# Dilated attention: probabilities and values as f32 operands of one product, instead of f16 halves in three

## The chip, the cores and the metric

The kernel runs on one core of a Trainium2 chip. The metric is the device time of one execution in microseconds (us). The core has a matrix engine (PE, whose weight loads the profile lists apart as PEld), a vector engine (DVE), a scalar engine (ACT), GpSimd (POOL) and a queue engine (SP), each with its own instruction stream; semaphores order them against each other. Matmuls read SBUF and write into the banks of PSUM, and ACT and DVE read those banks out.

## The reference

One residual layer on x of 1024 tokens by 1024 channels, all in f32. A normalised input is projected to 9232 columns; from these come a mixture of three dilated sliding-window attentions (8 heads of 64 in each of three groups), a gated delta rule, and gates that merge the two. The change lies in the attention:

```python
def _dilated_window_attention(q, k, v, window, dilation):
    ...
    scores = jnp.einsum('brnqhd,brnkhd->brnhqk', qb, kb) * (dh ** -0.5)
    ...                                             # causal mask and window
    m = jnp.max(scores, axis=-1, keepdims=True)
    p = jnp.exp(scores - m)
    den = jnp.sum(p, axis=-1, keepdims=True)
    o = jnp.einsum('brnhqk,brnkhd->brnqhd', p / den, vb)
    lse = (m + jnp.log(den))[..., 0].transpose(0, 1, 2, 4, 3)

def _dilated_mixture(q, k, v):
    ...                                             # one call for each of the three groups
    wts = jax.nn.softmax(jnp.stack(lses), axis=0)
    o = jnp.einsum('gbsh,gbshd->bshd', wts, jnp.stack(outs))
```

Queries and keys lie in blocks of 128; a block of queries meets its own block of keys and, where there is one, the block before.

## The kernel before, in words

Large products are made from f16 halves: an f32 operand is split into a high half and the f16 remainder, and three f16 products (high by high, high by low, low by high) are summed in PSUM. The helper `mm3_steps` (lines 183 to 185) issues them for the projections; `STT` and `TT` (lines 83 and 86) are short names of DVE operations, so many groups of the profile bear these two lines and are told apart by their tiles.

The projections are cut into units of 256 columns (q, k or v of four heads, a pair of gate columns, and so on). A `Feed` holds them in a list and hands them out a tick at a time, so that they can be interleaved with other work; a tick is one or a few steps of three products. PE's instructions stand in the order in which the program issues them. The instructions of DVE and ACT are put in order by a scheduler, which goes by priorities and its own estimates of when each can start.

The attention works on sets: a group g and a half of the heads hs, six in all, in the order (2,0), (2,1), (1,0), (1,1), (0,0), (0,1). The projection of a set's values is `v_unit`: for every two blocks of 128 tokens a PSUM bank of 512 columns is read out into `Vh` (by ACT, line 730) and `Vl` (by DVE, through `STT`), both f16. `att_run` goes through a set in 16 steps, one for each block of queries j and parity of the heads, two heads a step. It is a generator; between its parts the feed issues projections of the next units. A step has three parts, which run one step behind the other:

- `scores`: two products a head into a bank of "S" (lines 790 and 792), then on DVE the mask and the row maximum into `sm` (line 799), then on ACT the exponential and its row sums (line 803).
- `turn`: the probabilities are transposed by PE into a bank of "G" (line 813, f32, one turn for each head and block of keys); ACT copies them to `th` in f16 (line 818), and DVE writes the remainder `tl` (through `TT`, so line 86).
- `values`: for each head and each block of keys three products of 128 x 128 weights (`th`, `th`, `tl`) with 64 columns (`Vh`, `Vl`, `Vh`), lines 836, 838 and 840, into the one bank of "O". After the second parity ACT copies the bank to `osb` (line 845).

A block of queries has one block of keys in group 2, in the first block of each of the four strides of group 1, and in the first block of group 0; otherwise two. The results of groups 1 and 2 go to DRAM; in group 0 `combine` reads them back and mixes the three by their denominators, and later turns the result (line 899).

`Vh`, `Vl`, `sm`, `th` and `tl` lie in pools with two buffers a tag. In `rope_first` the slots of the values' tags are also lent to the first keys (`pkh`, `pkl`).

Of the kernel before, what the change touches and what calls it, by code (L numbers as in the profile page):

```python
# [10 lines left out]
F32 = mybir.dt.float32  # L11
F16 = mybir.dt.float16
BF16 = mybir.dt.bfloat16
AF = mybir.ActivationFunctionType
ALU = mybir.AluOpType
# [3 lines left out]
S = 1024  # L19
# [3 lines left out]
H_SCALE = 16.0  # L23
W_SCALE = 256.0
P_SCALE = 1.0 / (H_SCALE * W_SCALE)
# [52 lines left out]
def hybrid_block(ctx: ExitStack, tc: tile.TileContext, A):  # L78
    nc = tc.nc
    V, SC, PE, GP = nc.vector, nc.scalar, nc.tensor, nc.gpsimd  # L80

    def STT(out, in0, scalar, in1, op0, op1, eng=None):
        (eng or V).scalar_tensor_tensor(out, in0, scalar, in1, op0=op0, op1=op1)  # L83

    def TT(out, in0, in1, op, eng=None):
        (eng or V).tensor_tensor(out, in0, in1, op)  # L86
# [9 lines left out]
    start = [ctx.enter_context(ExitStack()) for _ in range(2)]  # L96
# [399 lines left out]
    with tc.manual_schedule(engines={nc.vector.engine, nc.scalar.engine}):  # L496
# [8 lines left out]
        pts = turn_rows(0)  # L505
# [11 lines left out]
        pts = turn_rows(1)  # L517
        split_rows(1, pts)
        rows_product(q, wq, 1, 0)
        pts = turn_rows(2)  # L520
# [12 lines left out]
        pts = turn_rows(3)  # L533
# [45 lines left out]
    ap = att.enter_context(tc.tile_pool(name="att", bufs=1, side="right"))  # L579
# [15 lines left out]
    def rope_room():  # L595
        return rp.tile([128, 2, 512], F32, name="rx", tag="rx", bufs=2)
# [37 lines left out]
    def rope_tiles():  # L634
        return {n: rp.tile([128, 2, S], F16, name=f"pc{n}", tag=f"pc{n}", bufs=1) for n in "hl"}
# [31 lines left out]

    def rope_first(g, ws, pieces):

        pts = [rope_tiles(), {n: ap.tile([128, 2, S], F16, name=f"pk{n}", tag="V" + n, bufs=2) for n in "hl"}]  # L670

        def half(pt, banks, hf, *offset):
            x = rope_room()
            for ct, p in enumerate(banks):
                rope_evict(g, x, p, ct, *offset)
            rope_half(g, pt, hf, x, *offset)

        for pt, banks in zip(pts, qk):
            half(pt, banks, 0, 0)
        ab = [q, [bank("S", 2), bank("S", 2)]]  # L680
        for i, u in ((2, 1), (3, 0), (3, 1)):
            for ct in range(2):
                quarter(ab[u][ct], ws[u], ct, i)
            if u == 0:

                with tc.high_priority():
                    for n in range(2):
                        feed.units[0][1].split(n)
        for pt, banks in zip(pts, ab):
            half(pt, banks, 1)  # L690
        for pt, pc in zip(pts, pieces):
            rope_out(pt, pc)
# [16 lines left out]

    def v_unit(g, tiles):  # L710
        def start():
            vs = [ap.tile([128, 8, 256], F16, name=n, tag=n, bufs=2) for n in ("Vh", "Vl")]
            tiles().extend(vs)
            return vs

        def gen(w):
            wh, wl = w
            Vh, Vl = start()
            for jj in range(4):
                p = bank("mm", 3)  # L720
                for u in range(2):
                    j = 2 * jj + u
                    for i, _ in enumerate(mm3_steps(
                            p[:, u * 256:u * 256 + 256], (lambda k: tok(g, h_hi, k, j), lambda k: tok(g, h_lo, k, j)),
                            (lambda k: wh[:, k], lambda k: wl[:, k]), first=(u == 0))):
                        if u == 1 and i == KT - 1:
                            with tc.high_priority():
                                vh = Vh[:, 2 * jj:2 * jj + 2].rearrange("p a b -> p (a b)")
                                vl = Vl[:, 2 * jj:2 * jj + 2].rearrange("p a b -> p (a b)")
                                SC.activation(vh, p, AF.Copy, scale=H_SCALE * P_SCALE)  # L730
                                STT(vl, p, H_SCALE * P_SCALE, vh, ALU.mult, ALU.subtract)
                        if i % 2:
                            yield

        def gen7(w):
            vs = start()

            def out(c, hf, p, rest):
                cs = slice(128 * c, 128 * c + 128)
                vh, vl = [v[:, 4 * hf:4 * hf + 4, cs] if g == 0 else  # L740
                          v.rearrange("p (r h) c -> p r h c", h=2)[:, :, hf, cs] for v in vs]
                p = p.rearrange("p (i c) -> p i c", c=128)
                with tc.high_priority():
                    if rest is not None:
                        rest = rest.rearrange("p (i c) -> p i c", c=128)
                        x = rope_room()[:, 0].rearrange("p (i c) -> p i c", c=128)
                        STT(x, p, -1.0, rest, ALU.mult, ALU.subtract)
                        p = x
                    SC.activation(vh, p, AF.Copy, scale=H_SCALE * P_SCALE)
                    STT(vl, p, H_SCALE * P_SCALE, vh, ALU.mult, ALU.subtract)  # L750

            yield from seven_products(w, out, by_token(g))

        return gen, gen7
# [2 lines left out]

    def att_run(g, hs, ts, pace):

        Qh, Ql, K, Vh, Vl = ts  # L760
        steps = [(j, par) for j in range(8) for par in range(2)]
        osbs, Ps, ths, pos = {}, {}, {}, {}
        if (g, hs) == sets[-1]:

            room = ap.tile([128, 2048], F32, name="osbs", tag="Ks", bufs=2)
# [40 lines left out]
        def turn(s):  # L806
            nk = len(blocks(steps[s][0]))
            P = Ps.pop(s)
            pt = bank("G", 2)
            for u in range(2):  # L810
                for i in range(nk):
                    c = (u * nk + i) * 128
                    PE.transpose(pt[:, c:c + 128], P[:, u, i * 128:i * 128 + 128], ident)  # L813
            n = 256 * nk
            th = ap.tile([128, 512], F16, name="th", tag="th", bufs=2)
            tl = ap.tile([128, 512], F16, name="tl", tag="tl", bufs=2)
            with tc.high_priority():
                SC.copy(th[:, :n], pt[:, :n])  # L818
                TT(tl[:, :n], pt[:, :n], th[:, :n], ALU.subtract)
            ths[s] = th, tl  # L820

        def values(s):
            j, par = steps[s]
            kb = blocks(j)
            nk = len(kb)
            th, tl = ths.pop(s)
            if par == 0:
                pos[j] = bank("O", 1)
            po = pos[j]
            for u in range(2):  # L830
                hd = 2 * u + par
                out = po[:, hd * 64:hd * 64 + 64]
                vs = slice(hd * 64, hd * 64 + 64)
                for i, b in enumerate(kb):
                    c = slice((u * nk + i) * 128, (u * nk + i) * 128 + 128)
                    PE.matmul(out, lhsT=th[:, c], rhs=Vh[:, b, vs], start=(hd == 0 and i == 0), stop=False,
                              skip_group_check=True)
                    PE.matmul(out, lhsT=th[:, c], rhs=Vl[:, b, vs], start=False, stop=False,
                              skip_group_check=True)
                    PE.matmul(out, lhsT=tl[:, c], rhs=Vh[:, b, vs], start=False, stop=(i == nk - 1),  # L840
                              skip_group_check=True)
            if par == 0:
                return
            osb = osbs.pop(j)
            SC.copy(osb[:, :256], po[:, :256])
            if g == 1:
                dst = dram[g, hs].rearrange("(n r) c -> r n c", r=4)[j // 2, 128 * (j % 2):128 * (j % 2) + 128]
                nc.scalar.dma_start(out=dst, in_=osb)
            elif g == 2:
                nc.scalar.dma_start(out=dram[g, hs].rearrange("(n r) c -> r n c", r=8)[j], in_=osb)  # L850
            else:
                feed.later(TURN_LAG, combine(hs, j, osb))

        n = len(steps)
# [11 lines left out]
    def combine(hs, j, osb):  # L866
# [8 lines left out]
        f = ap.tile([128, 3, 4], F32, name="f", tag="f", bufs=2)  # L875
        mx = ap.tile([128, 3, 4], F32, name="mx", tag="mx", bufs=2)
# [5 lines left out]
        TT(mx[:, 1], sml[:, 0], sml[:, 1], ALU.add)  # L882
        TT(mx[:, 1], mx[:, 1], sml[:, 2], ALU.add)
        V.reciprocal(mx[:, 2], mx[:, 1])
        STT(f, f, 1.0 / H_SCALE, mx[:, 2:3].to_broadcast([128, 3, 4]), ALU.mult, ALU.mult)

        def hv(x):
            return x.rearrange("p (h v) -> p h v", v=64)
# [88 lines left out]
    tiles = {}  # L977
# [93 lines left out]
    for t in range(8):  # L1071
        tk = slice(t * 128, t * 128 + 128)
        for k in range(KT):
            PE.matmul(pba[:, t * 32:t * 32 + 32], lhsT=h_hi[:, k, tk], rhs=wbas[:, k], start=(t == 0 and k == 0),
                      stop=False, skip_group_check=True)
            PE.matmul(pba[:, t * 32:t * 32 + 16], lhsT=h_lo[:, k, tk], rhs=wbas[:, k, 0:16], start=False,
                      stop=(k == KT - 1), skip_group_check=True)
# [595 lines left out]
    for t in range(8):  # L1673
# [373 lines left out]
```

## Time and profile before

| | |
|---|---|
| median of 3 runs | 1074.25 us (1074.08 to 1074.3) |
| profiled execution, its time | 1076.42 us |
| profiled execution, its span | 1074.6 us |
| mean granted clock of PE | 0.997 |
| attention steps (first turn to last value product) | 101.5 to 545.3 us |
| busy in the span | PE 1048.8, PEld 640.7, DVE 864.8, ACT 560.9, POOL 56.3 us |

The profile is of one execution. Each engine's busy time is the union of its instructions' records. A group is one line, engine, operation and pair of tiles, written as out<-in with its shape (partitions x elements) and type; behind it stand how often it ran, its busy time, the mean duration of one, and how long its engine was idle just before, with what ended that idle time. In the views in order of time a row gives the start, the duration, and the instructions that were merged into it. Line numbers are those of the kernel before.

### The profile page before, as it was taken

To read this page: it belongs to the slowest core of one execution; us is meant where nothing else is said; L and a number is where in the kernel's file an instruction comes from. 1 tells how busy PE (TensorE), PEld (TensorE's weight loads), DVE (VectorE), ACT (ScalarE), POOL (GpSimd) and SP (SyncE) were. 2 spreads that over 40 slices of the span, in tenths; PEclk is the share of its full clock that TensorE was granted. 3 is DMA by queue.
4 is the path that set the end of the run, shared out by engine and by line. 5 is a ranking of instruction groups with operands and counts; after the bars stand their busy time and mean duration, and the time that the engine had idled before them with its cause. 6 is when DMAs were issued, how large, how long until landed. Compare 5 with 4: busy or idle time off the path is not lost.

```text
span 1074.6 us, 23700 instructions
## 1 busy us (share of the span) xinstructions
PE 1048.8 (98%) x9410; PEld 640.7 (60%) x9410; DVE 864.8 (80%) x1986; ACT 560.9 (52%) x1274; POOL 56.3 (5%) x107
## 2 busy tenths in 40 slices
PE   7999999999999999999999999999999999999997
PEld 5994685775956855765645545555555555444444
DVE  6997997869879779979966997986488679899844
ACT  6455766566666656547735733234344346343523
POOL 0000000000000000000000000110200000000000
PEclk9999999999999999999999999999999999999999
DMA  8144531632625432641234357786685433763132
GB/s 278 60 133 103 139 104 54 171 98 87 181 69 154 108 103 63 177 115 46 76 123 165 84 130 205 237 240 164 184 267 174 140 99 116 286 209 123 48 131 79
DMA packets 99776, 148.47 MB, mean 138 GB/s; under 512 B 31168, under 2 KB 64704, under 8 KB 98512
## 3 DMA queue, kind: packets, MB, share of 16 engines
q1 hardware_dynamic: 69264, 84.64, 27.3%
q0 software_dynamic: 12320, 44.11, 13.1%
q10 hardware_dynamic: 18080, 18.20, 4.9%
q8 instruction: 74, 1.21, 0.5%
q14 instruction: 38, 0.31, 0.1%
HBM read 91.13 MB, written 36.90 MB: 119 GB/s over the span
## 4 chain that ended last, share of the span: by engine, by line
PE 60%; DVE 27%; ACT 5%; issue 3%; DMA 3%; SPq 1%; ACTq 0%; DVEq 0%
PE ps_mm L183 14%; PE ps_mm L184 14%; PE ps_mm L185 14%; DVE ca L83 4%; DVE wlo L83 2%; DVE X L86 2%; DVE stmp L86 2%; DVE sm L799 2%; PE ps_S L185 2%; PE ps_S L184 2%; PE ps_S L183 2%; DVE tl L86 1%; PE ps_G L813 1%; DVE rt L86 1%; ACT sm L803 1%
## 5 line engine op out<-in xcount | busy, mean ns | idle before, releaser
L185 PE MATMUL ps_mm<-h_hi,wlo 128*128 128x512 f16 (+1 forms) x552 | 207.9, 377 | 0.0
L183 PE MATMUL ps_mm<-h_hi,whi 128*128 128x512 f16 (+1 forms) x492 | 185.5, 377 | 0.0
L184 PE MATMUL ps_mm<-h_lo,whi 128*128 128x512 f16 (+1 forms) x492 | 185.3, 377 | 0.0
L185 PEld LDWEIGHTS <-wlo 128*128 128x128 f16 x788 | 77.2, 98 | 86.5 <-issue 0.7
L183 PEld LDWEIGHTS <-whi 128*128 128x128 f16 x848 | 83.3, 98 | 69.1 <-issue 0.6
L184 PEld LDWEIGHTS <-whi 128*128 128x128 f16 x848 | 83.1, 98 | 67.9 <-issue 0.9
L183 PE MATMUL ps_mm<-whi,h_hi 128*128 128x256 f16 x384 | 105.1, 274 | 0.0
L185 PE MATMUL ps_mm<-whi,h_lo 128*128 128x256 f16 x384 | 104.7, 273 | 0.0
L184 PE MATMUL ps_mm<-wlo,h_hi 128*128 128x256 f16 x384 | 104.7, 273 | 0.0
L803 ACT ACTIVATE sm<-sm,osb 128x128 f32<-128x128 f32 (+1 forms) x160 | 69.5, 435 | 65.3 <-DVE osb L799 58.7
L86 DVE TENSOR_TENSOR tl<-ps_G,th 128x256 f16<-128x256 f32 (+1 forms) x96 | 51.8, 539 | 22.1 <-ACT th L818 21.6
L799 DVE CUSTOM_DVE_ANT_0 sm<-ps_S,amask 128x128 f32<-128x128 f32 (+1 forms) x192 | 59.2, 345 | 6.0 <-PE ps_S L792 5.9
L83 DVE SCALAR_TENSOR_TENSOR wlo<-wstage,whi 128x1024 f16<-128x1024 f32 x50 | 60.9, 1217 | 3.4 <-ACT whi L166 3.2
L83 DVE SCALAR_TENSOR_TENSOR ca<-xc,cw,ca 128x512 f32<-128x512 f32 x72 | 53.8, 747 | 5.5 <-ACT ca L1010 4.8
L166 ACT ACTIVATE whi<-wstage 128x1024 f16<-128x1024 f32 x49 | 51.4, 1051 | 1.7 <-ACT gst L948 0.8
L813 PE MATMUL ps_G<-cons,sm 128*128 128x128 f32 x280 | 47.9, 275 | 3.2 <-ACT sm L803 1.5
L83 DVE SCALAR_TENSOR_TENSOR whi<-wstage,whi 128x512 f16<-128x512 f32 x60 | 40.8, 687 | 12.3 <-ACT whi L330 11.7
L330 ACT ACTIVATE whi<-wstage 128x512 f16<-128x512 f32 x60 | 37.1, 626 | 19.6 <-DVE wstage L329 13.3
L813 PEld LDWEIGHTS ps_G<-cons,sm 128*128 128x128 f32 x280 | 35.5, 141 | 19.4 <-ACT sm L803 5.0
L184 PEld LDWEIGHTS <-h_hi 128*128 128x128 f16 x384 | 45.8, 119 | 1.6
L183 PE MATMUL ps_mm<-h_hi,wlo 128*128 128x512 f16 x120 | 45.6, 380 | 1.0 <-DVE rx L83 1.0
L183 PEld LDWEIGHTS <-h_hi 128*128 128x128 f16 x384 | 45.5, 119 | 1.5
(459 smaller groups left out, 2595.7 us busy)
## 6 DMA issues: line engine op xcount, KB each, us to landing
wstage<-in_w POOLq DMA_DIRECT2D x68, 512.0 KB, 4.5
og<-osb ACTq DMA_DIRECT2D x32, 132.0 KB, 2.2
og<-og SPq DMA_DIRECT2D x32, 132.0 KB, 2.2
gspb<-gst ACTq DMA_DIRECT2D x16, 256.0 KB, 2.4
sga<-gspa SPq DMA_DIRECT2D x8, 512.0 KB, 6.5
wstage<-in_w_up POOLq DMA_DIRECT2D x8, 512.0 KB, 4.7
wos<-in_w_out SPq DMA_DIRECT2D x8, 512.0 KB, 5.3
sgb<-gspb SPq DMA_DIRECT2D x8, 512.0 KB, 4.9
```

Source lines behind the costliest of these rows:

```text
L83: (eng or V).scalar_tensor_tensor(out, in0, scalar, in1, op0=op0, op1=op1)
L86: (eng or V).tensor_tensor(out, in0, in1, op)
L166: in_turn(SC.activation(hi[:, 4 * c:4 * c + 4], st, AF.Copy, scale=W_SCALE))
L183: PE.matmul(out, lhsT=wh(k), rhs=mh(k), start=first and i == 0, stop=False, skip_group_check=True)
L184: PE.matmul(out, lhsT=wh(k), rhs=ml(k), start=False, stop=False, skip_group_check=True)
L185: last_pe[0] = PE.matmul(out, lhsT=wl(k), rhs=mh(k), start=False, stop=last and i == len(ks) - 1, skip_group_check=True).ins.name
L330: in_turn(SC.activation(t[:, b, 0], self.part[name], AF.Copy, scale=W_SCALE))
L799: V.tensor_tensor_reduce(P[:, u, :128 * nk], psc[:, u * 256:u * 256 + 128 * nk], mask, -cexp, -NEG, ALU.add, ALU.min, accum_out=osb[:, 256 ...
L803: SC.activation(P[:, u, :128 * nk], P[:, u, :128 * nk], AF.Exp, bias=osb[:, 256 + hd:257 + hd], scale=-1.0, accum_out=osb[:, 260 + hd:261 ...
L813: PE.transpose(pt[:, c:c + 128], P[:, u, i * 128:i * 128 + 128], ident)
```

## The change

The values are copied out of PSUM once, in f32 and without a factor, into a tile `vals` that is as large as `Vh` and `Vl` together. The turned probabilities are copied once, in f32, into `PT`, as large as `th` and `tl` together. For each head and block of keys one f32 product takes the place of three f16 products. The factor that the values lacked is put into the mixing weights of `combine`. The first keys borrow the slot of `vals`, cut in two by a view.

```diff
-        pts = [rope_tiles(), {n: ap.tile([128, 2, S], F16, name=f"pk{n}", tag="V" + n, bufs=2) for n in "hl"}]
+        pk = ap.tile([128, 8, 256], F32, name="pk", tag="vals", bufs=2).rearrange("p a b -> p (a b)").bitcast(F16)
+        pk = pk.rearrange("p (l a s) -> p l a s", l=2, a=2)
+        pts = [rope_tiles(), {n: pk[:, i] for i, n in enumerate("hl")}]
...
-            vs = [ap.tile([128, 8, 256], F16, name=n, tag=n, bufs=2) for n in ("Vh", "Vl")]
-            tiles().extend(vs)
-            return vs
+            v = ap.tile([128, 8, 256], F32, name="vals", tag="vals", bufs=2)
+            tiles().append(v)
+            return v
...
-                                SC.activation(vh, p, AF.Copy, scale=H_SCALE * P_SCALE)
-                                STT(vl, p, H_SCALE * P_SCALE, vh, ALU.mult, ALU.subtract)
+                                SC.copy(v[:, 2 * jj:2 * jj + 2].rearrange("p a b -> p (a b)"), p)
...
-            th = ap.tile([128, 512], F16, name="th", tag="th", bufs=2)
-            tl = ap.tile([128, 512], F16, name="tl", tag="tl", bufs=2)
+            PT = ap.tile([128, 512], F32, name="PT", tag="PT", bufs=2)
             with tc.high_priority():
-                SC.copy(th[:, :n], pt[:, :n])
-                TT(tl[:, :n], pt[:, :n], th[:, :n], ALU.subtract)
+                SC.copy(PT[:, :n], pt[:, :n])
...
-                    PE.matmul(out, lhsT=th[:, c], rhs=Vh[:, b, vs], start=(hd == 0 and i == 0), stop=False,
-                              skip_group_check=True)
-                    PE.matmul(out, lhsT=th[:, c], rhs=Vl[:, b, vs], start=False, stop=False,
-                              skip_group_check=True)
-                    PE.matmul(out, lhsT=tl[:, c], rhs=Vh[:, b, vs], start=False, stop=(i == nk - 1),
+                    PE.matmul(out, lhsT=PT[:, c], rhs=vals[:, b, vs], start=(hd == 0 and i == 0), stop=(i == nk - 1),
                               skip_group_check=True)
...
-        STT(f, f, 1.0 / H_SCALE, mx[:, 2:3].to_broadcast([128, 3, 4]), ALU.mult, ALU.mult)
+        STT(f, f, P_SCALE, mx[:, 2:3].to_broadcast([128, 3, 4]), ALU.mult, ALU.mult)
```

On PE the order of everything else stays. In a step of set (0,1), behind a projection's last product, there stood the following rows; the six rows from L836 on stand once for each head and block of keys (four times in a step with two blocks), and the projections go on behind them.

```order
L185 LDWEIGHTS wlo
L185 MATMUL ps_mm<-h_hi,wlo 128x512
L836 LDWEIGHTS th
L836 MATMUL ps_O<-Vh,th 128x64
L838 LDWEIGHTS th
L838 MATMUL ps_O<-Vl,th 128x64
L840 LDWEIGHTS tl
L840 MATMUL ps_O<-Vh,tl 128x64
```

Now, at a step with two blocks, the order has this (an f32 matmul issues its weight loads itself, and they have no rows of their own here):

```order
L185 LDWEIGHTS wlo
L185 MATMUL ps_mm<-h_hi,wlo 128x512
L830 MATMUL ps_O<-vals,PT 128x64 x4
L183 LDWEIGHTS whi
L183 MATMUL ps_mm<-h_hi,whi 128x512
```

So 840 products with 840 loads became 280 products, in 52 groups of two and 44 of four, at the same places.

On DVE the split `tl` went out of 96 places and `Vl` out of 24, and the scheduler put the rest in another order. At the end of set (0,0), where the results of the groups are mixed (`og`, `osb`, `f`), DVE had:

```order
L86 TENSOR_TENSOR og<-og,f 128x256 x2
L86 TENSOR_TENSOR tl<-ps_G,th 128x512
L86 TENSOR_TENSOR osb<-osb,f 128x256
L86 TENSOR_TENSOR og<-og,f 128x256
L86 TENSOR_TENSOR osb<-osb,og 128x256
L86 TENSOR_TENSOR og<-og,f 128x256
L86 TENSOR_TENSOR osb<-osb,og 128x256
L86 TENSOR_TENSOR osb<-osb,f 128x256
L86 TENSOR_TENSOR osb<-osb,og 128x256 x2
L86 TENSOR_TENSOR tl<-ps_G,th 128x512
L83 SCALAR_TENSOR_TENSOR Vl<-ps_mm,Vh 128x512
```

and has now:

```order
L86 TENSOR_TENSOR og<-og,f 128x256 x2
L86 TENSOR_TENSOR osb<-osb,f 128x256
L83 SCALAR_TENSOR_TENSOR wlo<-wstage,whi 128x1024
L86 TENSOR_TENSOR osb<-osb,og 128x256
L795 ISA sm,osb<-ps_S,amask 128x256
L795 ISA osb 128x1
L795 ISA sm,osb<-ps_S,amask 128x256
L795 ISA osb 128x1
L86 TENSOR_TENSOR osb<-osb,og 128x256
```

The two splits are gone from there; the split of a unit's weights (`wlo`) and the mask and maximum of the next step's scores (line 795 of the changed kernel, 799 before) stand between parts of the mixing.

More of the change, by code (lines that the diff above doesn't have):

```diff
@@ L711, in start @@
         def start():
-            vs = [ap.tile([128, 8, 256], F16, name=n, tag=n, bufs=2) for n in ("Vh", "Vl")]
-            tiles().extend(vs)
-            return vs
+            v = ap.tile([128, 8, 256], F32, name="vals", tag="vals", bufs=2)
+            tiles().append(v)
+            return v
         def gen(w):
             wh, wl = w
-            Vh, Vl = start()
+            v = start()
             for jj in range(4):
@@ L727, in gen @@
                             with tc.high_priority():
-                                vh = Vh[:, 2 * jj:2 * jj + 2].rearrange("p a b -> p (a b)")
-                                vl = Vl[:, 2 * jj:2 * jj + 2].rearrange("p a b -> p (a b)")
-                                SC.activation(vh, p, AF.Copy, scale=H_SCALE * P_SCALE)
-                                STT(vl, p, H_SCALE * P_SCALE, vh, ALU.mult, ALU.subtract)
+                                SC.copy(v[:, 2 * jj:2 * jj + 2].rearrange("p a b -> p (a b)"), p)
                         if i % 2:
@@ L735, in gen7 @@
         def gen7(w):
-            vs = start()
+            v = start()
             def out(c, hf, p, rest):
                 cs = slice(128 * c, 128 * c + 128)
-                vh, vl = [v[:, 4 * hf:4 * hf + 4, cs] if g == 0 else
-                          v.rearrange("p (r h) c -> p r h c", h=2)[:, :, hf, cs] for v in vs]
+                dst = (v[:, 4 * hf:4 * hf + 4, cs] if g == 0 else
+                       v.rearrange("p (r h) c -> p r h c", h=2)[:, :, hf, cs])
                 p = p.rearrange("p (i c) -> p i c", c=128)
                 with tc.high_priority():
[L744 to L750, printed above, removed]
+                    if rest is None:
+                        SC.copy(dst, p)
+                    else:
+                        STT(dst, p, -1.0, rest.rearrange("p (i c) -> p i c", c=128), ALU.mult, ALU.subtract)
             yield from seven_products(w, out, by_token(g))
@@ L758, in att_run @@
     def att_run(g, hs, ts, pace):
-        Qh, Ql, K, Vh, Vl = ts
+        Qh, Ql, K, vals = ts
         steps = [(j, par) for j in range(8) for par in range(2)]
-        osbs, Ps, ths, pos = {}, {}, {}, {}
+        osbs, Ps, PTs, pos = {}, {}, {}, {}
         if (g, hs) == sets[-1]:
@@ L814, in turn @@
             n = 256 * nk
-            th = ap.tile([128, 512], F16, name="th", tag="th", bufs=2)
-            tl = ap.tile([128, 512], F16, name="tl", tag="tl", bufs=2)
+            PT = ap.tile([128, 512], F32, name="PT", tag="PT", bufs=2)
             with tc.high_priority():
-                SC.copy(th[:, :n], pt[:, :n])
-                TT(tl[:, :n], pt[:, :n], th[:, :n], ALU.subtract)
-            ths[s] = th, tl
+                SC.copy(PT[:, :n], pt[:, :n])
+            PTs[s] = PT
         def values(s):
@@ L825, in values @@
             nk = len(kb)
-            th, tl = ths.pop(s)
+            PT = PTs.pop(s)
             if par == 0:
```

## The prediction

> **What bounds the kernel now.** I read the head of the page first, then the busy time by stage, then the matmul groups, the order in time around one attention step, and last the waits of PE.
>
> ```profile
> span 1074.6 us, 23700 instructions
> PE 1048.8 (98%) x9410; PEld 640.7 (60%) x9410; DVE 864.8 (80%) x1986; ACT 560.9 (52%) x1274; POOL 56.3 (5%) x107
> ...
> PE 60%; DVE 27%; ACT 5%; issue 3%; DMA 3%; SPq 1%; ACTq 0%; DVEq 0%
> ```
>
> PE is busy for 98% of the span. The chain that ended last gives DVE 27%, but a chain only follows who released whom; whether DVE really holds PE up is read from PE's idle time by stage. All attention steps lie between 100 and 546 us:
>
> ```profile
> 100.00:546.00 446.00, 438.54 (x3723) 300.39 (x3721) 378.79 (x1029) 284.80 (x770) 18.54 (x35) 1.00 0.38 107
> 546.00:1075.00 529.00, 518.16 (x4786) 264.01 (x4784) 401.49 (x827) 222.07 (x418) 32.68 (x59) 0.99 0.52 161
> ```
>
> The columns are length, then busy PE, weight loads, DVE, ACT, POOL, and then the granted clock, 1.00. In the attention stretch PE lacks only 446.0 - 438.5 = 7.5 us of being busy, while DVE lacks 67 and ACT 161. PE executes in order, so each microsecond that its instructions get longer there is a microsecond of the end, and each that DVE saves is worth at most PE's small idle time. A record of a matmul includes the end of its pipeline, so the price of a product is not its mean duration but the distance between starts:
>
> ```profile
> L838 PE MATMUL ps_O<-Vl,th 128*128 128x64 f16 x280 | 35.0, 193 | 0.0
> L836 PE MATMUL ps_O<-Vh,th 128*128 128x64 f16 x280 | 34.9, 193 | 0.5 <-ACT osbs L845 0.5
> L840 PE MATMUL ps_O<-Vh,tl 128*128 128x64 f16 x280 | 34.7, 193 | 2.7 <-DVE tl L86 2.7
> ...
> 490.66 0.19 PE L836 MATMUL ps_O<-Vh,th 128*128 128x64 f16 x1
> ...
> 490.83 0.38 PE L183 MATMUL ps_mm<-h_hi,whi 128*128 128x512 f16 x1
> ...
> 498.60 0.19 PE L836 MATMUL ps_O<-Vh,th 128*128 128x64 f16 x1
> ...
> 498.95 0.38 PE L183 MATMUL ps_mm<-h_hi,whi 128*128 128x512 f16 x1
> ```
>
> There are 3 x 280 products, each 193 ns in its record. But the six of a step with one block of keys (two heads) run from 490.66 to the next projection at 490.83, 0.17 us, and the twelve of a step with two blocks from 498.60 to 498.95, 0.35 us: 29 ns each.
>
> **The change part by part.** How many steps are of which kind is told by the split that is removed, which runs once a step:
>
> ```profile
> L86 DVE TENSOR_TENSOR tl<-ps_G,th x96: 393/425/692, 102.9 to 544.2; 128x256 f16<-128x256 f32 x52, 128x512 f16<-128x512 f32 x44
> L86 DVE TENSOR_TENSOR tl<-ps_G,th 128x256 f16<-128x256 f32 (+1 forms) x96 | 51.8, 539 | 22.1 <-ACT th L818 21.6
> L83 DVE SCALAR_TENSOR_TENSOR Vl<-ps_mm,Vh x24: 678/690/693, 70.1 to 470.3; 128x512 f16<-128x512 f32 x24
> L730 ACT ACTIVATE Vh<-ps_mm x24: 573/594/598, 66.6 to 469.7; 128x512 f16<-128x512 f32 x24
> ```
>
> 52 steps have one block and 44 have two: 52 x 2 + 44 x 4 = 280 products a kind, as above.
>
> First, what goes from PE: 52 x 0.17 + 44 x 0.35 = 24.2 us.
>
> Second, what comes to PE: 280 products with f32 weights of 128 x 128 (the turned probabilities) and 64 f32 columns of values. The kernel before has that very shape in two calls next to each other, where the decay sums are made, and again with a single moving column in the first norm:
>
> ```profile
> 500.46 0.41 PEld L1120 LDWEIGHTS ps_G<-bg,cons 128*128 128x128 f32 x2
> 500.68 0.33 PE L1120 MATMUL ps_G<-bg,cons 128*128 128x64 f32 x2
> 500.79 0.30 PEld L1121 LDWEIGHTS ps_G<-bg,cons 128*128 128x128 f32 x2
> 500.85 0.39 PE L1121 MATMUL ps_G<-bg,cons 128*128 128x64 f32 x2
> 501.07 0.38 PE L183 MATMUL ps_mm<-h_hi,whi 128*128 128x512 f16 x1
> ...
> 28.56 0.56 PE L415 MATMUL ps_G<-cons,xt 128*128 128x1 f32 x4
> 28.98 0.61 PE L478 MATMUL ps_S<-h_hi,whi 128*128 128x128 f16 x8
> ```
>
> Each call stands as x2: one f32 product is two weight loads and two matmuls. The pair of calls takes from 500.68 to 501.07, 0.39 us, with its first load already made under the projection before (the load starts at 500.46); the second call alone, with nothing to hide its loads, takes 0.85 to 1.07, 0.22 us. With one column in place of 64 a pair of calls takes just as long, 28.56 to 28.98, 0.42 us. So the moving columns do not set the price; the loads of f32 weights do, at about 0.11 us each. A step with one block holds two such products (0.39 us), a step with two blocks four (0.39 + 2 x 0.22 = 0.83 us): 52 x 0.39 + 44 x 0.83 = 56.8 us. Against the 24.2 removed that is +32.6 us on PE.
>
> The Trainium skill has a rule that speaks against the change in the same place: TensorE: Matmul & The Clock Gate, "Weight-path perf modes", says that the fast load of weights is on for 128 weights of a type other than FP32, and its section on LDWEIGHTS gives the load without it as the number of columns over 1.2 GHz, 107 ns for 128. By that figure, an estimate, 280 products x 2 loads x 107 ns are 59.9 us and the sum on PE +35.7 in place of +32.6; the rows differ from it by the load that each step hides under the matmul ahead of it.
>
> Third, the bounds of that price. From above: no step hides its first load, each product 0.22 us: 61.6 - 24.2 = +37.4. From below: the loads are hidden altogether and only the moving columns count. The nearest rows for that are the f32 turns of the probabilities, four of 128 columns in 0.44 us:
>
> ```profile
> 489.57 0.60 PE L813 MATMUL ps_G<-cons,sm 128*128 128x128 f32 x4
> 490.01 0.38 PE L183 MATMUL ps_mm<-h_hi,whi 128*128 128x512 f16 x1
> ```
>
> That is 110 ns for 128 columns, 55 ns for 64, two matmuls a product: 280 x 0.11 = 30.8, or +6.6 us. I take +32.6, since L1120 and L1121 have the shape, the types and the neighbours of the new products, and the turns have neither the two-part weights nor the same kind of load.
>
> Fourth, ACT. The 96 copies out of PSUM stay, with an f32 output in place of f16, and so do the 24 of the values.
>
> ```profile
> 483.78 0.58 ACT L1008 COPY xc<-ps_mm 128x512 f32<-128x512 f32 x1
> ...
> 486.57 0.37 ACT L818 CAST th<-ps_G 128x256 f16<-128x256 f32 x1
> ...
> 500.18 0.37 ACT L845 COPY osbs<-ps_O 128x256 f32<-128x256 f32 x1
> ```
>
> A copy of 256 columns is 0.37 us to f16 and to f32 alike, one of 512 is 0.58 to f32 against the 0.59 of Vh. I cost this at nothing; ACT's 161 us of idle time would hide a small difference.
>
> Fifth, DVE loses 51.8 us (tl) and 24 x 0.69 = 16.6 us (Vl), 68 of its 379 in this stretch. What that is worth is what PE waits for:
>
> ```profile
> PE ps_O L840 <- DVE tl L86: 2.7, 3, 1.3
> PE ps_G L813 <- ACT sm L803: 1.5, 4, 0.6
> PE ps_G L813 <- DVE tl L86: 1.2, 1, 1.2
> PE ps_mm L183 <- DVE rx L83: 1.0, 1, 1.0
> PE ps_O L836 <- ACT osbs L845: 0.5, 1, 0.5
> PE ps_G L813 <- ACT osbs L900: 0.2, 1, 0.2
> ```
>
> That is 7.1 us in 11 waits. In each the start comes some 0.16 us later still than the row says, because the record of the matmul ahead runs on by its pipeline (193 ns against the 29 ns of its turn). The four waits for tl go with their cause: 3.9 + 4 x 0.16 = 4.5 us. Late next at those places is th, now PT, which ACT writes before tl is begun, so the whole wait goes. The other seven, 3.2 + 7 x 0.16 = 4.3 us, come from ACT and from a DVE that is less loaded while PE takes longer; between none and all of it I take half, 2.1. Together -6.6, with 0 and -8.8 as ends.
>
> DMA, POOL and SP: nothing is added or taken away, and the tiles keep their sizes and numbers of buffers. The order of all other PE instructions is the same, so after 546 us the work is only shifted; the 11 us that PE lacks there belong to waits that the change does not touch.
>
> The sum: +32.6 - 6.6 = +26.0 us. The profiled execution had a span of 1074.6 and a time of 1076.42; it becomes a span of 1100.6 and a time of 1102.4. The median of the runs, 1074.25, lies 2.2 below the profiled time, and becomes 1100.3.
>
> **The rivals.**
>
> The loads are hidden, and the kernel is a little faster. If PE can pull the second load of an f32 product under the matmul ahead, as it does for the turns, the change costs +6.6, and if all 8.8 us of waits go, the time is 1072.1; with 6.6 of waits gone it is 1074.3, no change. It decides from a product below (24.2 + 8.8) / 280 = 0.118 us. For it speaks the turns' 110 ns; against it L1121 with 0.22 us and L415, which takes as long with one column. The Trainium skill, FP8 and Floating Point Precision, "TensorE Precision Notes", counts true FP32 as four passes, and read as four passes of columns alone at the 29 ns of the f16 products this gives an estimate of 0.117 us a product, the same case; the one-column row disagrees with that reading.
>
> Full price and no wait regained: +37.4, 1111.7. It would need the first load of each step to come late too. The waits for tl speak against it, since their cause is gone.
>
> New waits. With tl gone the scheduler has put DVE's other work in another order; in one place the mask and row maximum of the next scores now stand behind a 1024-column split of weights and parts of the mixing of groups. If once in each of the 16 steps of one set PE waited 0.6 us for sm (the longest such wait above), 16 x 0.6 = 9.6 would be added: 1109.9. DVE's 67 us of idle time, now about 135 and more, speak against it.
>
> More is taken in. If all 8.8 us of waits go and, besides, half of the 10.8 us that PE lacks after 546 goes, because DVE and the DMAs come there with a lead: +32.6 - 8.8 - 5.4 = +18.4, 1092.7. Nothing in the change reaches that far, and those waits follow on one another there.
>
> That the change does not do what it says is no case: 280 products in 52 groups of two and 44 of four stand in PE's order where 840 stood.
>
> **How the numbers follow.** The likeliest case, 1100.3, has 0.79, full price 0.05, new waits 0.07, more taken in 0.04, loads hidden 0.05. A change of 0.2%, about 2.1 us, is the least that the measurement tells from none. All but the last are slower: 0.95. The last I split into 0.03 faster and 0.02 the same. The range goes from the case of more taken in to that of the full price, 1092 to 1112, which leaves out the loads hidden and little else.
>
> **What would show it.** In the profile of the changed kernel the value products should stand as 560 loads and 560 matmuls of 64 f32 columns, in place of 840 and 840, with 0.39 us from the first of a two-product step to the next projection, and about 0.83 for a four-product step; PE's records should number 9130. DVE's busy time should fall to some 797 us with tl and Vl gone, and PE's waits for DVE should be below 3 us before the attention ends. That end should come at about 572 in place of 546, and from there to the end of the span the time should be as before. I would be wrong if a four-product step took near 0.45 us (the loads are hidden), or if PE's waits for sm grew to several microseconds.

## The result, and the profile after

The changed kernel takes 1102.06 us (median of four runs, 1100.25 to 1104.07), the kernel before 1074.28 beside it: the ratio is 1.0253, 95% interval 1.0228 to 1.0278. It is slower by 2.5%, some 27 us. The profiled execution took 1102.46 us with a span of 1100.7.

The head of its page, and the busy time by stage (length, PE, weight loads, DVE, ACT, POOL, clock), cut where the attention ends:

```profile
span 1100.7 us, 23034 instructions
PE 1077.9 (98%) x9130; PEld 679.3 (62%) x9130; DVE 814.1 (74%) x1866; ACT 566.5 (51%) x1274; POOL 56.4 (5%) x107
...
100.00:572.00 472.00, 471.33 (x3463) 340.40 (x3461) 337.91 (x939) 293.47 (x776) 18.76 (x36) 1.00 0.37 103
572.00:1100.00 528.00, 514.65 (x4772) 262.54 (x4770) 394.58 (x802) 219.72 (x413) 32.48 (x59) 0.99 0.51 160
```

In the attention PE now lacks 0.7 us of being busy, where it lacked 7.5. DVE lacks 134. The attention is bound by PE alone.

The value products by line, then a step with two products and one with four in order of time, each with the projection behind it:

```profile
L830 PE MATMUL ps_O<-vals,PT x560: 219/275/323, 105.7 to 568.2; 128*128 128x64 f32 x187
...
105.75 0.55 PE L830 MATMUL ps_O<-vals,PT 128*128 128x64 f32 x4
106.14 0.38 PE L183 MATMUL ps_mm<-h_hi,whi 128*128 128x512 f16 x1
...
522.94 1.00 PE L830 MATMUL ps_O<-vals,PT 128*128 128x64 f32 x8
523.78 0.38 PE L183 MATMUL ps_mm<-h_hi,whi 128*128 128x512 f16 x1
```

The two-product step takes 105.75 to 106.14, 0.39 us, the four-product step 522.94 to 523.78, 0.84 us. Over all steps, from the starts in the trace, the products take 57.4 us; the f16 products took 24.4 without their waits (medians 0.174 and 0.349 us, 52 and 44 steps). That is +33.0.

What PE waits for between 100 and 572 us is down to one row, in place of the six before:

```profile
PE ps_G L809 <- ACT sm L799: 0.6, 1, 0.6
```

That one wait stands at 102 us, ahead of the first value product; before there was one like it at 101.5.

The first value product starts at 105.1 us before and 105.7 after, the last at 545.3 and 568.2: that stretch grew from 440.2 to 462.5, by 22.3 us. So of the 33.0 on PE, 10.7 came back there. Behind the attention, from the last value product to the end of the span, it takes 532.5 us in place of 529.3. That lies in one wait, of which the row before and the row after are:

```profile
PE ps_S L1266 <- ACT uw L1424: 2.3, 1, 2.3
...
PE ps_S L1256 <- ACT uw L1414: 5.4, 1, 5.4
```

### The profile page after: what moved, and what is told of

Its sections match the earlier page's. It is cut to its first block, busy times and chain, and to the rows that moved or that the text cites. A ratio compares the mean times of both kernels' runs of the same rounds, so it can differ in the third digit from the quotient of the medians.

```text
span 1100.7 us, 23034 instructions
## 1 busy us (share of the span) xinstructions
PE 1077.9 (98%) x9130; PEld 679.3 (62%) x9130; DVE 814.1 (74%) x1866; ACT 566.5 (51%) x1274; POOL 56.4 (5%) x107
## 4 chain that ended last, share of the span: by engine, by line
PE 80%; DVE 13%; ACT 3%; DMA 2%; issue 2%; ACTq 0%; SPq 0%; DVEq 0%
PE ps_mm L183 19%; PE ps_mm L185 18%; PE ps_mm L184 18%; PE ps_O L830 5%; DVE ca L83 3%; PE ps_G L809 3%; DVE X L86 2%; DVE stmp L86 2%; PE ps_S L183 2%; PE ps_S L185 2%; PE ps_S L184 2%; PE ps_S L788 1%; PE ps_S L786 1%; DVE wlo L83 1%; PE ps_G L185 1%
## 5 line engine op out<-in xcount | busy, mean ns | idle before, releaser
L183 PEld LDWEIGHTS <-whi 128*128 128x128 f16 x848 | 85.7, 101 | 69.8 <-issue 1.2
L184 PEld LDWEIGHTS <-whi 128*128 128x128 f16 x848 | 83.1, 98 | 67.5 <-issue 0.3
L830 PEld LDWEIGHTS ps_O<-vals,PT 128*128 128x128 f32 x560 | 74.4, 191 | 8.1
L830 PE MATMUL ps_O<-vals,PT 128*128 128x64 f32 x560 | 73.1, 266 | 0.0
L813 ACT COPY PT<-ps_G 128x256 f32<-128x256 f32 (+1 forms) x96 | 44.3, 461 | 11.4 <-PE ps_G L809 10.9
```

Source lines behind the costliest of these rows:

```text
L183: PE.matmul(out, lhsT=wh(k), rhs=mh(k), start=first and i == 0, stop=False, skip_group_check=True)
L184: PE.matmul(out, lhsT=wh(k), rhs=ml(k), start=False, stop=False, skip_group_check=True)
L813: SC.copy(PT[:, :n], pt[:, :n])
L830: PE.matmul(out, lhsT=PT[:, c], rhs=vals[:, b, vs], start=(hd == 0 and i == 0), stop=(i == nk - 1), skip_group_check=True)
```

## The experiments

Each run was timed beside the kernel before, in three rounds. The stretch from the first to the last value product is called the attention's stretch: 440.2 us before, 462.5 changed.

**Wider moving operands.** Is the price set by the loads or by the columns? Each product takes 128 columns of values, of which 64 are used:

```diff
-                out = po[:, hd * 64:hd * 64 + 64]
-                vs = slice(hd * 64, hd * 64 + 64)
+                out = po[:, hd * 128:hd * 128 + 128]
+                vs = slice(hd // 2 * 128, hd // 2 * 128 + 128)
```

> The changed kernel with 128 moving columns in each f32 product in place of 64 (the values of a pair of heads; the half that is not wanted goes to unused columns of the bank, and ACT copies the wanted ones out in two pieces). Theory (the loads of f32 weights set the pace, 112 ns a record as long as the two passes of columns need no more): a two-product step stays at 0.39 us, a four-product step at 0.84, time 1100 to 1105. Rival (the moving columns set it): each product 0.11 us longer, 280 x 0.11 = 31, about 1133.

Measured 1103.33 us, ratio 1.0265 (1.0248 to 1.0282). A two-product step in order of time:

```profile
105.64 0.61 PE L830 MATMUL ps_O<-vals,PT 128*128 128x128 f32 x4
106.09 0.38 PE L183 MATMUL ps_mm<-h_hi,whi 128*128 128x512 f16 x1
```

It takes 0.45 us in place of 0.39; the median of the four-product steps is 0.893 in place of 0.838. Twice the columns add 0.054 us to a step, whatever its number of products. By the starts in the trace that is the first record of a step alone, whose load is made under the projection ahead: the second record follows it after 56 ns at 64 columns and after 110 at 128. All later ones follow after 112 ns in both kernels. So behind the first record the loads set the pace and the columns run beside them. The expectation was right on this, but its time was met by luck. The attention's stretch is 469.0 us (105.6 to 574.6), 6.5 more than in the changed kernel: 5.2 from the 0.054 us of 96 steps, the rest from waits. It was made up for by 5.6 us less behind the attention, of which more below.

Then 256 columns (`vs = slice(0, 256)`, a bank of "O" for each step, and ACT copies out the wanted 64 of each head):

> The changed kernel with 256 moving columns in each f32 product (the values of all four heads; a bank for every step, and ACT copies the wanted 64 of each head out). Theory (a record takes the longer of 112 ns for its load and 2 x 256 columns at 2.4 a ns, 216 ns): steps of 0.87 and 1.73 us, 52 x 0.87 + 44 x 1.73 = 121 in place of 57, so +64, about 1166. Rival one (only the loads count): no change, 1102. Rival two (cost goes with the columns from 64 on): four times 0.22 a product, +185, about 1287.

Measured 1162.11 us, ratio 1.0805 (1.0787 to 1.0823). A four-product step:

```profile
503.91 1.89 PE L828 MATMUL ps_O<-vals,PT 128*128 128x256 f32 x8
505.64 0.27 PE L183 MATMUL ps_mm<-whi,h_hi 128*128 128x256 f16 x1
```

1.73 us for eight records, 216 ns each, as expected; all steps together take 121.3 us. From 128 to 256 columns the columns have become the bound. The theory of loads has both its sides: flat up to 128 behind a step's first record, and at 256 columns the pace of twice the columns. That 1162 was measured and not 1166 lies behind the attention, where this run takes 3.6 us less than the changed kernel; the stretch grew by the 64 us expected.

**Narrower loads.** Each product is cut into two of 64 weight columns, the upper and lower half of the queries:

```diff
-                    PE.matmul(out, lhsT=PT[:, c], rhs=vals[:, b, vs], ...)
+                    for r in range(2):
+                        PE.matmul(out[64 * r:64 * r + 64], lhsT=PT[:, c.start + 64 * r:c.start + 64 * r + 64],
+                                  rhs=vals[:, b, vs], ...)
```

> The changed kernel with each f32 product cut into two of 64 weight columns (the upper and the lower half of the queries), 64 moving columns each; the result is the same. Theory (a load costs in proportion to its weight columns, and loads and columns of the two halves of the array go one after the other): 4 records of 56 ns a product in place of 2 of 112, no change, 1100 to 1104. Rival one (the halves of the array work side by side, as in the rows of line 1107, where eight records of 128 x 64 weights took 0.38 us): 0.19 us a product, about 1094. Rival two (a load costs 0.11 us whatever its width): 0.45 us a product, +63, about 1164.

Measured 1097.73 us, ratio 1.0213 (1.0196 to 1.0230). A two-product step with the projections around it:

```profile
506.57 0.38 PE L184 MATMUL ps_mm<-h_lo,whi 128*128 128x512 f16 x1
506.79 0.38 PE L185 MATMUL ps_mm<-h_hi,wlo 128*128 128x512 f16 x1
507.10 0.45 PE L831 MATMUL ps_O<-vals,PT 128*64 128x64 f32 x8
507.48 0.39 PE L183 MATMUL ps_mm<-h_hi,whi 128*128 128x512 f16 x1
```

The halves do work side by side: a step takes 0.38 us with two products and 0.62 with four, so a product more costs 0.117 us in place of 0.224. But entering costs: the projection ahead holds PE from 506.79 to 507.10, 0.31 us, where it takes 0.22 elsewhere, and 25.2 us over the 96 steps where it was 16.4. The records just behind the steps cost 1.6 us more in all. So the 57.4 us became 47.1 + 8.8 + 1.6 = 57.5, and nothing is left of the gain: the attention's stretch is 462.5 us (105.2 to 567.7), as in the changed kernel. The 4 us by which this run is faster lie behind it, where PE waits 2.4 us for uw and not 5.4, and in the granted clock there (below). So the expected time of rival one nearly came, but not for its reason; its 0.19 us a product holds for a two-product step only. (The eight records it took this from are those of lines 1107 and 1113 together.)

**DVE's load put back.** After each copy DVE subtracts it from its bank, in place:

```diff
                 SC.copy(PT[:, :n], pt[:, :n])
+                TT(pt[:, :n], pt[:, :n], PT[:, :n], ALU.subtract)
...
+                                STT(p, p, 1.0, vv, ALU.mult, ALU.subtract)
```

> The changed kernel with DVE's old load put back: after each copy of PT and of vals DVE subtracts the copy from its PSUM bank, in place, 96 and 24 times as tl and Vl before; nothing reads the result, but the bank comes free only behind it. Theory (PE's waits for tl went because no product waits for a DVE result any more, and because PE's steps are longer; DVE's load by itself costs little): waits of PE in the attention 0 to 2 us, time 1100 to 1105, as the changed kernel. Rival (the relief of DVE by 68 us is what gave the 8 us back): the waits return through the banks, 1107 to 1111.

Measured 1101.55 us, ratio 1.0241 (1.0222 to 1.0259). Its busy time by engine, and by stage over the attention:

```profile
PE 1078.1 (98%) x9130; PEld 678.3 (62%) x9130; DVE 869.3 (79%) x1986; ACT 566.8 (52%) x1274; POOL 56.2 (5%) x107
...
100.00:569.00 469.00, 468.83 (x3450) 339.19 (x3448) 384.80 (x1036) 291.83 (x773) 18.51 (x35) 1.00 0.37 103
```

DVE is as busy as before, 869 us, and PE lacks 0.2 us in 469. The stretch is 462.6 (105.2 to 567.8). So it is not the relief of DVE that gave the 10.7 us back. The rival falls. Moreover the orders of DVE and ACT are nearly those of the kernel before here: the splits set aside, 19 of DVE's 1866 rows and 8 of ACT's 1274 stand at another place, against 460 and 214 in the changed kernel. So a new order is not needed for it either.

**The splits gone, the f16 products kept.** `tl` and `Vl` are not made, and the three products take `th` and `Vh`:

```diff
-                TT(tl[:, :n], pt[:, :n], th[:, :n], ALU.subtract)
-            ths[s] = th, tl
+            ths[s] = th, th
...
-                                STT(vl, p, H_SCALE * P_SCALE, vh, ALU.mult, ALU.subtract)
```

> The kernel before, with its three f16 products a head and block, but without the two splits on DVE (tl and Vl): the products take th and Vh three times, and the mixing divides by three, so the low halves are left out of the result. PE's instructions are as many and as long as before. Theory (the change gives back the waits of PE because DVE is relieved and tl is not waited for): all 7.1 us of waits in the attention and their 0.16 us tails go, some 7 to 9 us, 1065 to 1067. Rival one (only the four waits for tl go, the others come from ACT and the order of the work): -4.5, about 1070. Rival two (DVE's splits hold nothing up, the waits come back elsewhere): 1073 to 1075.

Measured 1069.17 us, ratio 0.9943 (0.9925 to 0.9961). PE's waits in the attention:

```profile
PE ps_O L1071 <- ACT osb L842: 1.6, 1, 1.6
PE ps_G L812 <- ACT sm L802: 1.4, 2, 0.8
PE ps_O L833 <- ACT osbs L842: 0.4, 1, 0.4
```

The stretch is 435.0 us (105.1 to 540.1): -5.2. Every wait for DVE is gone, and PE now waits 3.4 us for ACT. Rival one's 1070 was nearer than my 1065 to 1067. With f16 steps half of the 10.7 us is all that the splits were worth; in 3.4 us of this stretch, from 466.1 us on, the granted clock was 0.5, which cost some 0.6 us by the starts in the trace.

The other half can be read from this run beside the changed kernel. Neither makes the splits, and their orders are nearly the same (45 of DVE's rows and 18 of ACT's stand at another place). From one to the other the value products grow by 33.0 us, and the stretch from 435.0 to 462.5, by 27.5. So 5.5 us come back here with the longer f32 steps, of which the 0.6 of the clock are no wait.

**PE's time alone.** If it is the time of those steps alone that removes the other half, f16 products that take as long should do the same. Four more for each head and block of keys, into columns that nobody reads:

```diff
+                    for m in range(4):
+                        PE.matmul(po[:, 256 + hd * 64:320 + hd * 64], lhsT=th[:, c], rhs=Vh[:, b, vs], start=False,
+                                  stop=True, skip_group_check=True)
```

> The kernel before, splits on DVE and all, with four more f16 products for each head and block of keys, into columns of the bank that nobody reads: seven products of 29 ns are 0.20 us, 57.2 us in all, what the f32 products take. Theory (the change is a matter of PE's time: longer steps on PE give ACT and DVE the time for which PE waited before): +33 on PE, and of the 10 us that the changed kernel gained from waits at least 5 are gained here too, 1097 to 1102. Rival (the waits go only where tl is gone): the waits for tl stay, 1104 to 1107.

Measured 1109.45 us, ratio 1.0320 (1.0302 to 1.0339): slower than either expectation. The products take 57.0 us (medians 0.407 and 0.815), as planned, but the stretch grew by 29.4 (105.3 to 574.9), so only 3.2 us of waits went. Another 3.9 us came behind the attention (533.2 in place of 529.3). What stays in the attention:

```profile
PE ps_G L813 <- ACT sm L803: 2.4, 3, 1.1
PE ps_G L813 <- ACT osbs L903: 1.4, 2, 0.9
PE ps_O L840 <- DVE tl L86: 0.5, 1, 0.5
PE ps_O L836 <- ACT osbs L848: 0.4, 1, 0.4
PE ps_G L813 <- DVE tl L86: 0.3, 1, 0.3
```

The waits for tl fell from 3.9 to 0.8 us, as longer steps should make them; but waits for ACT rose. The scheduler had put DVE's and ACT's instructions into another order here (456 of DVE's 1866 rows and 226 of ACT's 1274 stand at another place than in the kernel before). To keep that order and let no product wait for tl, the product that read tl was made to read `th` into the unused columns (`range(5)`), while DVE still makes tl:

> As the run with seven f16 products, but the product that took tl takes th and goes to the unused columns; DVE still makes tl, in the same place of its order (DVE and ACT have the same orders as in that run), and nothing reads it. The low half of the probabilities is left out of the result. That run took 1109.5 where the f32 products, with the same time on PE and DVE's load kept, took 1101.6. Theory (PE's waiting for tl itself, and what it delays, is the difference): 1100 to 1103. Rival (the order into which the scheduler put DVE and ACT in that run is the difference; the waits for tl were only 0.8 us there): 1107 to 1110, with PE's waits for sm and osbs as they were.

Measured 1108.01 us (1105.40 to 1111.41), ratio 1.0314 (1.0286 to 1.0341). The stretch is 470.3 us (105.8 to 576.1), and PE still waits 2.2 us for sm and 2.2 for osbs. The waits for DVE did not go either:

```profile
PE ps_G L900 <- DVE tl L86: 0.8, 1, 0.8
PE ps_G L813 <- DVE tl L86: 0.3, 1, 0.3
```

No product reads tl here, but a turn into a bank of "G" still waits until DVE has read that bank. So the run took away the value products' waiting for tl and no more. With the same orders on DVE and ACT the same stretch comes back, whether a product reads tl or not: my theory falls. For the longest wait for sm, 1.15 us (1.14 in the run before this one), the trace shows the order to be the cause. ACT's rows ahead of that exponential here, and of the same one in the run with DVE's load put back:

```profile
120.39 0.39 ACT L803 ACTIVATE sm<-sm,osb 128x128 f32<-128x128 f32 x1
...
121.55 1.05 ACT L604 COPY rx<-ps_mm 128x512 f32<-128x512 f32 x1
122.40 0.63 ACT L974 CAST sum5h<-hx 128x512 f16<-128x512 f32 x1
122.92 0.40 ACT L803 ACTIVATE sm<-sm,osb 128x128 f32<-128x128 f32 x1
...
120.11 0.40 ACT L801 ACTIVATE sm<-sm,osb 128x128 f32<-128x128 f32 x1
120.39 0.20 ACT L801 ACTIVATION_READ_ACCUMULATOR sm<-sm,osb 128x1 f32 x1
120.49 0.40 ACT L801 ACTIVATE sm<-sm,osb 128x128 f32<-128x128 f32 x1
```

In the one the second head's exponential stands behind other work of ACT and starts 2.5 us after the first head's, though DVE had its row maximum ready at 119.9; in the other it follows at once. For the rest of the 7 us between 462.6 and 469.6 the order is the likely, not the shown, cause: that order was not put on the f32 kernel, and the f32 kernels of this study, in five orders, have at most 1.5 us of waits in the attention.

**A second profile.** The changed kernel again, unaltered:

> The changed kernel, unaltered, for a second profile. In its first profile PE waited 5.4 us for ACT's copies uw, at about 789 us, against 2.3 before, and all of the time lost behind the attention was there. Theory (that wait hangs on when DMAs land and differs from one execution to the next): 1.5 to 3.5 us this time, and the rest of the profile as in the first one, with 23 us gained by PE's clock of events up to the end of the attention. Rival (the change moves those DMAs to a worse phase): 5 us again. Time 1100 to 1104.

Measured 1101.21 us, ratio 1.0248 (1.0231 to 1.0265). The stretch is 462.4, as in the first profile. The wait for uw was 4.1 us, longer than I expected and shorter than the rival did. Over the profiles of this study that wait, the granted clock around it and the time from the last value product to the end of the span go together:

| kernel | PE waits for uw, us | granted clock at 0.5 in or just behind that wait, us | last value product to end, us |
|---|---|---|---|
| 128 columns | 2.0 | 0 | 526.9 |
| half weights | 2.4 | 0 | 527.2 |
| splits gone | 2.6 | 0 | 527.4 |
| seven, tl not read | 2.4 | 0 | 528.2 |
| 256 columns | 2.4 | 0 | 528.9 |
| before | 2.3 | 3.4 | 529.3 |
| DVE's load put back | 2.4 | 3.4 | 529.8 |
| changed, second profile | 4.1 | 6.8 | 531.6 |
| changed, first profile | 5.4 | 6.8 | 532.5 |
| one f16 product (below) | 4.7 | 6.8 | 533.0 |
| seven f16 products | 4.5 | 6.8 | 533.2 |

Four of the eleven have the longer wait, among them two f16 kernels, and two kernels with the same orders on DVE and ACT (seven products, tl read or not) fall on different sides. So it is not a cost of the f32 products. The wait alone does not give the last column: before and half weights wait equally long. The clock is the other part. The rows below are of the changed kernel's first profile and of the one with half weights, some 7 us around the wait or behind it; the clock is the third number from the right, 0.50 and 1.00. Then come two projections of the first of these stretches:

```profile
786.10:792.80 6.70, 3.49 (x66) 2.38 (x67) 1.47 (x3) 1.22 (x2) 0.00 (x0) 0.50 0.38 116
785.00:792.00 7.00, 6.99 (x148) 4.12 (x149) 5.18 (x9) 2.09 (x4) 0.98 (x2) 1.00 0.49 166
...
791.63 0.63 PE L184 MATMUL ps_mm<-h_lo,whi 128*128 128x512 f16 x1
792.05 0.63 PE L185 MATMUL ps_mm<-h_hi,wlo 128*128 128x512 f16 x1
```

At a clock of 0.5 a projection's product takes 0.42 us from start to start, where it takes 0.22 elsewhere. In the four profiles with the longer wait the clock fell when PE had waited for 1.8 to 3.2 us, and in the two with 3.4 us it fell behind the wait. In the changed kernel the longer wait and the longer low clock came in both profiles. What chooses them is open.

**A version that beats both.** The run without splits still made three products of the same two operands. One is enough for them:

```diff
-                    PE.matmul(out, lhsT=th[:, c], rhs=Vl[:, b, vs], start=False, stop=False, ...)
-                    PE.matmul(out, lhsT=tl[:, c], rhs=Vh[:, b, vs], start=False, stop=(i == nk - 1), ...)
```

> One f16 product, th by Vh, for each head and block of keys, without the two splits; the low halves are left out of the result. It should beat both kernels. From the run without the splits (1069.2): 560 products of 29 ns less, -16.3. Theory (PE's time is the end's time, and waits come back as PE's steps get shorter): 1053 to 1058, with PE's waits in the attention above the 3.8 us of that run. Rival (DVE and ACT become the bound of the attention): 1060 or more.

Measured 1059.57 us, ratio 0.9853 (0.9833 to 0.9874), 1.5% faster than before. The products take 8.1 us. PE's waits:

```profile
PE ps_G L812 <- ACT sm L802: 2.7, 5, 0.8
PE ps_O L833 <- ACT osbs L838: 1.2, 3, 0.5
PE ps_O L1067 <- ACT osb L838: 0.4, 1, 0.4
```

The stretch is 420.2 us (105.1 to 525.3), 14.8 less than with three products for 16.3 less on PE: 4.3 us of waits in place of 3.4, so PE is still the bound. The time is just above my 1053 to 1058, since this profile is one of those with the longer wait for uw and 6.8 us of half the clock (533.0 behind the attention, against 527.4 in the run without splits). It is a kernel of f16 probabilities and values, without their low halves.

## Why the prediction was right

The forecast was 1100.3 us; 1102.06 was measured, inside 1092 to 1112. Point by point:

- What bounds it: PE's order and its gapless stream in the attention. It held; 33.0 us were put on PE, and nothing else grew there.
- The price of a product: 0.39 and 0.83 us a step, 56.8 in all, against 0.391, 0.838 and 57.4. The pair L1120 and L1121 was the product itself, and the row with one column had told that behind a load the columns do not count. The runs with 128 and 256 columns show where they begin to, and that a step's first record, with its load made ahead, does pay for its columns. The rule of the Trainium skill that was weighed there (TensorE: Matmul & The Clock Gate, LDWEIGHTS) agrees: 107 ns a load, 112 measured from record to record.
- The removal: 24.2 us, measured 24.4.
- ACT and the copies at nothing: ACT's busy time is 566.5 in place of 560.9, and PE waits 0.6 us for it, ahead of the first value product. It held.
- The waits: -6.6, with 0 and -8.8 as ends. The term was too small: 10.7 us came back. Ten of the eleven waits of the list went, 6.5 us and ten times 0.16, which makes 8.1, and some 2.6 us more that the list of waits before does not show. The reason given for the part from ACT, a less loaded DVE, is not what did it: with DVE's load put back the same 10.7 us are gained. What is shown is that the f32 steps run without waits whether DVE splits or not, that the splits alone are worth 5.2 us with f16 steps, and that f16 steps of the same length, in another order of DVE and ACT, get only 3.2 us back.
- After 546 us only a shift: true of the work, but the first profile has 3.2 us more there, in the wait for uw. This made up for most of what the waits were better by: 33.0 - 10.7 + 0.6 at the start + 3.2 = 26.1, the difference of the spans. That the sum of +26.0 was met so closely is therefore luck in part: the term for the waits was 4.1 us off, and 3.8 us that the prediction did not have cancelled it.
- DVE's busy time was to be 797 us and is 814: records on DVE overlap (those of the kernel before sum to 982 us, and their union is 865), and the union that the page counts fell by 51 us where the removed records sum to 68.

Of the rivals, "the loads are hidden" (0.118 us a product) did not come for 128 weight columns; with 64 a further product did cost 0.117, but going into and out of products of half the width took the gain away. "New waits" and "more is taken in" did not come in the attention.

## What to carry to other kernels

Before trading f16 halves for f32 look for an f32 product of the same shape in the trace and measure from start to start: here one f32 product cost 0.224 us against 0.088 for three f16 products, because each of its two loads takes 112 ns and the moving side was only 64 columns wide. With 128 moving columns the same loads carried twice the columns for 6% more time in a four-product step; with 256 the time of a step nearly doubled as well. Where PE is the bound, instructions saved on another engine count only through the waits of PE, and those waits depend on the whole order of the other engines, so they are better measured by a run than summed from a list.

## What the runs showed of the hardware

A record of an f32 matmul with 128 weight columns starts 112 ns after the one ahead of it at 1, 64 and 128 moving columns, and 216 ns after it at 256. A step's first record, whose load was made under the projection, is followed sooner: after 56 ns at 64 columns and 110 at 128. With 64 weight columns in both halves of the array, two records start 7 ns apart and the next pair 58 ns later (107 behind the first pair), so the halves load and compute side by side. Those 58 ns are near the 56 of the columns above, so this run does not tell what a load of 64 weight columns costs by itself. Going from products of the whole array into such a group held PE for 94 ns (0.309 us from the last projection to the first record, against 0.215). The first load of the group starts only then, at 507.10 in the step shown, where that of a whole-array f32 step starts with the projection ahead. The Trainium skill, TensorEngine Tiling (Array Packing), "Key Properties", says that a change of tiling mode drains the engine; this trace fits that, and puts a number on the way in, but it does not show the drain itself.
